# A decoder step on one Trainium2 core: the second norm's chain reordered, unread products in its wait, and the dt steps spaced out

## The chip, the core and the metric

The kernel runs as one program on one core of a Trainium2 chip. The core has five engines with instruction queues of their own: TensorE (PE; its weight loads are shown as PEld), VectorE (DVE), ScalarE (ACT), GpSimd (POOL) and SyncE (SP, which here only starts transfers). They meet in on-chip memory (SBUF) and in eight accumulator banks (PSUM), and wait for one another by semaphores. The metric is the device time of one execution in microseconds. The kernel before took 1796.03 us, the median of 3 runs (1794.56 to 1798.4).

## What is computed

One step of a hybrid decoder layer for 256 prompt tokens and 64 sample tokens (8 sequences of 8), 320 columns in all, with model width 2048:

```python
h   = rms_norm(x, norm_mix_pre)
proj = h @ w_in                       # gate u, gate v, SSD z, SSD x/B/C, dt
mix = concat([gate(u, v), ssd(z, conv(xBC), dt)]) @ w_out
x   = x + rms_norm(mix, norm_mix_post)            # "second norm"
f   = conv_ffn(rms_norm(x, norm_ffn_pre))         # w_up, causal conv, gelu(g) * u, w_down
x   = x + rms_norm(f, norm_ffn_post)              # last norm
```

`rms_norm(x, w)` divides each token's row by the root of the mean of its squares (plus 1e-6) and scales by `w`. The SSD scan also returns its state for the prompt and for each sample sequence. All is in float32.

## The kernel before

Activations lie transposed, with 128 features on the partitions and the 320 tokens along the free axis, so the model width is sixteen blocks ("columns" k = 0 to 15 of `hT`, `acc`). Float32 precision is got from three products of a faster format: a weight slab `wraw` (128 x 1024) is loaded by SP, ScalarE casts it to its high part `whi` (L118), VectorE subtracts to get the low part `wlo` (L120), and `accumulate` (L127 to L131) issues whi x h_hi, whi x h_lo and wlo x h_hi, each 128 x 128 by 320 columns. Slabs, high and low parts have three buffers each; the next slab is loaded when both parts of an older one are made, and a part's buffer is free when PE has used it.

`project` (L153) multiplies `hT` by the columns of a weight matrix. Up to k = 12 it takes slabs of two k-blocks for four output blocks, and with `more` also slabs of four k-blocks for two more outputs (L191 to L193); so four k-blocks are 72 products. `chunk_out` (L205) multiplies one chunk of mixed features by `w_out` or `w_down` and adds the result to `acc` on VectorE (L217). `squares_of` (L284) squares each finished block and adds it to a running total; the last blocks go by VectorE, the very last stays by itself.

Around the second norm (L1013 to L1028) the order is written out by hand with `tc.issue_after`, which places an instruction behind another one in the order of its engine: behind the last product of the output projection come the two state products of `grown` (L834) with their additions (L836) and stores from POOL's queue (L841), the sums by token of the total and of the last square (`token_sums`, L263), the product of the prompt state (`final`, L938) with its addition (L940) and store (L941), the root and one Newton step (`rsqrt_by_root`, L249 to L255), and `spread` (L271), three transposes that bring the root back to the transposed layout.

`x1_ready` (L1037) is called by `project(ffn_w_up, ...)` one slab ahead. For each k it multiplies `acc` by the norm's weight and the spread root (L1042), adds the residual `xr` (L1043; on VectorE for k = 0 and 1, on POOL for the others), and splits the result into `h_hi` (ScalarE, L346) and `h_lo` (VectorE, L347). When `k % 4 == 3` it asks for the next block of the residual on SP. The third norm needs the squares of the new `acc` (L1051 to L1053), which VectorE adds up; their sums by token stand in PE's order behind the first product of `ps_one` (L1107 to L1115).

`steps` (L411) is a generator for the SSD's step sizes, ticked along with the projections: sums over the decay (`cs_ps` L473, `csT_ps` L488, `dec_ps` L501) follow the softplus of dt on VectorE (L449 to L465), with exponentials on ScalarE (L484, L510, L514). Between its yields, other work is put in.

A scheduler outside the kernel orders each engine's instructions by priority (`first()` and `high_priority` raise it) and by its own estimates, so a change at one place can reorder neighbours.

## Time and profile before

| | us |
|---|---|
| median of 3 runs | 1796.03 (1794.56 to 1798.4) |
| the profiled execution's own time | 1796.18 |
| its span, first to last instruction | 1794.3 |
| PE busy | 1774.6 |
| VectorE busy | 1185.2 |
| ScalarE busy | 797.8 |
| POOL busy | 293.2 |
| mean granted clock of TensorE | 0.996 |
| PE's longest waits: for the last norm's additions | 2.4 in 2 |
| for the second norm's first split | 2.1 in 1 |

In rows of a timeline the first number is the start from the beginning of the span, the second the length, then engine, line, operation, output and inputs with shapes; brackets hold the idle time ahead of it and what ended that. Neighbouring rows of one kind are merged (x2). In rows of windows the stretch is followed by its length, the busy time of the engines asked for with the number of instructions touching it, the granted clock of TensorE as a share of full, the share of time the transfer engines were busy, and GB/s. Products overlap on PE, so the spacing of their starts, and not their length, is what one costs.

### The profile page before, as it was taken

What the parts mean: (1) busy time and instruction counts of PE and PEld (TensorE: products, weight loads), DVE (VectorE), ACT (ScalarE), POOL (GpSimd) and SP (SyncE); (2) the same over time, 40 slices, a digit from 0 to 9 for tenths busy, and PEclk for the clock granted to TensorE, in tenths of its full rate; (3) what the DMA queues carried; (4) which work ended last, traced back from release to release, by engine and by line L of the source; (5) the groups of instructions that cost most, each with busy time, mean ns of one, the idle gap of its engine ahead of it and who ended that gap; (6) DMA issues with size and microseconds to landing.
All of it is one profiled execution on the core that took longest, in us unless ns stands there. A gap on an engine that the chain in (4) does not pass through costs nothing.

```text
span 1794.3 us, 31172 instructions
## 1 busy us (share of the span) xinstructions
PE 1774.6 (99%) x12200; PEld 1741.1 (97%) x12200; DVE 1185.2 (66%) x2048; ACT 797.8 (44%) x1107; POOL 293.2 (16%) x619
## 2 busy tenths in 40 slices
PE   9999999999999999999999999999999999999998
PEld 8999999999889898999999999999999999999997
DVE  5459664556987969677875474746566575656575
ACT  6444454334545446445555433343434343433335
POOL 3102200000431303104321010111101020101004
PEclk9999999999999999999999999999999999999999
DMA  8646544445665565554554545554554555454542
GB/s 279 193 142 192 161 145 153 154 153 180 198 196 187 166 222 163 172 170 145 167 156 154 151 147 155 154 151 148 155 153 146 152 155 152 149 150 154 153 150 101
DMA packets 222226, 292.56 MB, mean 163 GB/s; under 512 B 16672, under 2 KB 150656, under 8 KB 221888
## 3 DMA queue, kind: packets, MB, share of 16 engines
q1 hardware_dynamic: 209392, 268.12, 49.1%
q10 hardware_dynamic: 10304, 14.82, 2.3%
q0 software_dynamic: 2384, 7.64, 1.4%
q8 instruction: 96, 1.57, 0.4%
q14 instruction: 50, 0.41, 0.1%
HBM read 275.71 MB, written 14.82 MB: 162 GB/s over the span
## 4 chain that ended last, share of the span: by engine, by line
PE 91%; DVE 4%; DMA 3%; issue 1%; ACT 1%; POOL 0%; DVEq 0%; ACTq 0%; POOLq 0%
PE ps L129 20%; PE ps L131 19%; PE ps L130 19%; PE pd L129 9%; PE pd L131 9%; PE pd L130 9%; DMA wraw<-in_w_in 1%; DVE wlo L120 1%; DMA cs<-dacs_d 1%; PE y_ps L912 1%; PE yo_ps L817 0%; PE sg L670 0%; DVE cv L388 0%; PE up_ps L834 0%; DVE cs L897 0%
## 5 line engine op out<-in xcount | busy, mean ns | idle before, releaser
L120 DVE TENSOR_TENSOR wlo<-wraw,whi 128x1024 fp32r<-128x1024 f32 (+1 forms) x474 | 585.4, 1235 | 434.0 <-ACT whi L118 431.9
L118 ACT CAST whi<-wraw 128x1024 fp32r<-128x1024 f32 (+1 forms) x475 | 494.8, 1042 | 715.9 <-PE ps L130 431.5
L129 PE MATMUL ps<-h_hi,whi 128*128 128x320 f32 x2524 | 783.4, 311 | 4.8 <-ACT h_hi L346 2.1
L131 PE MATMUL ps<-h_hi,wlo 128*128 128x320 f32 x2524 | 781.3, 310 | 2.0 <-DVE wlo L120 1.9
L130 PE MATMUL ps<-h_lo,whi 128*128 128x320 f32 x2524 | 780.8, 309 | 0.0
L129 PEld LDWEIGHTS ps<-h_hi,whi 128*128 128x128 f32 x2524 | 475.1, 188 | 8.8 <-issue 2.9
L131 PEld LDWEIGHTS ps<-h_hi,wlo 128*128 128x128 f32 x2524 | 474.9, 188 | 3.8 <-DVE wlo L120 3.1
L130 PEld LDWEIGHTS ps<-h_lo,whi 128*128 128x128 f32 x2524 | 475.2, 188 | 0.7 <-DVE h_lo L546 0.2
L129 PE MATMUL pd<-fhi,whi 128*128 128x320 f32 x704 | 217.5, 309 | 0.0
L130 PE MATMUL pd<-flo,whi 128*128 128x320 f32 x704 | 217.5, 309 | 0.0
L131 PE MATMUL pd<-fhi,wlo 128*128 128x320 f32 x704 | 217.5, 309 | 0.0
L129 PE MATMUL pd<-ohi,whi 128*128 128x320 f32 x448 | 139.8, 312 | 0.0
L131 PE MATMUL pd<-ohi,wlo 128*128 128x320 f32 x448 | 138.8, 310 | 0.0
L130 PE MATMUL pd<-olo,whi 128*128 128x320 f32 x448 | 138.6, 309 | 0.0
L129 PEld LDWEIGHTS pd<-fhi,whi 128*128 128x128 f32 x704 | 132.4, 188 | 0.0
L130 PEld LDWEIGHTS pd<-flo,whi 128*128 128x128 f32 x704 | 132.4, 188 | 0.0
L131 PEld LDWEIGHTS pd<-fhi,wlo 128*128 128x128 f32 x704 | 132.4, 188 | 0.0
L1093 POOL COPY ptf<-pad 128x2 f32<-128x2 f32 x88 | 21.0, 239 | 622.3 <-DVE pad L1081 621.6
L217 DVE TENSOR_TENSOR acc_ffn<-acc_ffn,pd 128x320 f32<-128x320 f32 x160 | 77.5, 484 | 38.3 <-PE pd L131 36.9
L129 PEld LDWEIGHTS pd<-ohi,whi 128*128 128x128 f32 x448 | 84.1, 188 | 1.4 <-issue 0.6
L131 PEld LDWEIGHTS pd<-ohi,wlo 128*128 128x128 f32 x448 | 84.1, 188 | 0.5 <-issue 0.4
L130 PEld LDWEIGHTS pd<-olo,whi 128*128 128x128 f32 x448 | 84.1, 188 | 0.2
(301 smaller groups left out, 1590.3 us busy)
## 6 DMA issues: line engine op xcount, KB each, us to landing
wraw<-in_ffn_w_up SPq DMA_DIRECT2D x176, 512.0 KB, 3.7
wraw<-in_w_in SPq DMA_DIRECT2D x144, 512.0 KB, 3.7
wraw<-in_ffn_w_down SPq DMA_DIRECT2D x88, 512.0 KB, 3.5
wraw<-in_w_out SPq DMA_DIRECT2D x64, 512.0 KB, 3.5
st<-in_state_ssm SPq DMA_DIRECT2D x32, 256.0 KB, 4.1
out_ssm_state_sample<-st ACTq DMA_DIRECT2D x30, 256.0 KB, 3.5
cs<-dacs_d SPq DMA_DIRECT2D x16, 320.0 KB, 4.2
xr<-in_xT SPq DMA_DIRECT2D x4, 640.0 KB, 3.9
```

What stands on the lines that cost most here:

```text
L118: act.copy(hi[:, o], raw[:, o])
L120: dve.tensor_tensor(out=lo[:, :m], in0=raw[:, :m], in1=hi[:, :m].bitcast(F32), op=ALU.subtract)
L129: pe.matmul(ps, whi, xhi, start=first, stop=False)
L130: pe.matmul(ps, whi, xlo, start=False, stop=False)
L131: return pe.matmul(ps, wlo, xhi, start=False, stop=last).ins
L217: dve.tensor_tensor(out=acc[:, nb, :], in0=acc[:, nb, :], in1=ps[:, :NT], op=ALU.add)
L912: pe.matmul(ps[64 * i:64 * i + 64, cols], w(hl), x(hl, m, cpx), tile_position=(0, 64 * i), **flags)
L1093: pool.tensor_copy(ptf[:, k, :], pad[:, 256:258])
```

## The change

1. In `chunk_out`, where block 15 is added at the end of a norm's last chunk, the addition is made in two parts (tokens 0 to 127, 128 to 319), and `squares_of` squares the two parts one by one. It concerns the second and the last norm.
2. The two state products of the last SSD group and their additions are placed behind the second part. The addition of the prompt state and its store move from between root and residual to behind the low part of k = 2.
3. The parts of the slab that feeds outputs 4 and 5 of the up projection (cast and subtraction) are placed behind the root and behind the low part of k = 1.
4. One product of 128 x 128 by 512 columns, whose result nobody reads, is placed behind the prompt state's product, and seven more behind the spread.
5. k = 1 is multiplied only after k = 0's residual is added; all residual additions are on VectorE.
6. The first k-block of the up projection is taken by parts: four products with whi x h_hi, four with wlo x h_hi, then four with whi x h_lo.
7. `steps` yields five times, not two, ahead of the sums over the decay, and once more between them.

```diff
@@ slab
+            late = split_after[-1]
+            with tc.issue_after(late[0]) if late else nullcontext(), tc.issue_after(late[1]) if late else nullcontext():
+                hi = wp.tile([P, 1024], F32R, tag="whi", name="whi", bufs=3)
...
+                dve.tensor_tensor(out=lo[:, :m], in0=raw[:, :m], in1=hi[:, :m].bitcast(F32), op=ALU.subtract)
@@ project / part
-            by_part = range(nk if ready and k0 == 0 and nk == 1 else 0)
+            by_part = range(1 if ready and k0 == 0 and nk < 4 else 0)
             for k in by_part:
-                for i in range(3):
+                for i in (0, 1, 2) if nk == 1 else (0, 2, 1):
...
                     if more and k0 % 4 == 2:
+                        if k0 == 2:
+                            split_after.append((rooted[-1], low[1]))
                         with tc.issue_after(held[1]):
                             part(rows_of(w, k0 - 2, 4, more, 256), k0 - 2, 4, (4, 5))
+                        split_after.append(None)
@@ chunk_out
+    def parts_of(nb):
+        return (slice(0, P), slice(P, NT)) if nb == KD - 1 else (slice(0, NT),)
...
-                    dve.tensor_tensor(out=acc[:, nb, :], in0=acc[:, nb, :], in1=ps[:, :NT], op=ALU.add)
+                    for ts in parts_of(nb) if done else (slice(0, NT),):
+                        added_last[:] = [dve.tensor_tensor(out=acc[:, nb, ts], in0=acc[:, nb, ts], in1=ps[:, ts], op=ALU.add).ins]
@@ squares_of
-                act.activation((one or held)[-1], acc[:, nb, :], AF.Square)
+                for ts in parts_of(nb):
+                    act.activation((one or held)[-1][:, ts], acc[:, nb, ts], AF.Square)
@@ steps
-            yield
-            yield
+            for _ in range(5):
+                yield
...
                 act.activation(ed[s_at], p4[s_at, :, r], AF.Exp)
+            yield
@@ the second norm
+            def idle_products(ps, n):
+                for _ in range(n):
+                    ins = pe.matmul(ps, bsp[:, 0, :P], bsp[:, 0, :], start=True, stop=True).ins
+                return ins
...
-                with tc.issue_after(pd_last[-1]):
+                with tc.issue_after(pd_last[-1]), tc.issue_after(added_last[0]):
                     made = rest[0]()
...
                 behind = rsqrt_ins[-1]
-                with tc.issue_after(behind):
-                    next(rest[1])
+                idle = misc("idle")
+                with tc.issue_after(made):
+                    made = idle_products(idle, 1)
                 with tc.issue_after(made):
                     r2b = spread(r)
+                with tc.issue_after(spread_ins[-1]):
+                    idle_products(idle, 7)
@@ x1_ready
-                        dve.scalar_tensor_tensor(out=a, in0=a, scalar=col(prm_at["norm"][0] + kt), in1=r2b, op0=ALU.mult, op1=ALU.mult)
-                        added.append((dve if kt < 2 else pool).tensor_tensor(out=a, in0=a, in1=xr[q][:, k, :], op=ALU.add).ins)
-                        split(hT[0][:, kt, :], hT[1][:, kt, :], a, col(prm_at["norm"][1] + kt))
+                        with tc.issue_after(added[0]) if kt == 1 else nullcontext():
+                            dve.scalar_tensor_tensor(out=a, in0=a, scalar=col(prm_at["norm"][0] + kt), in1=r2b, op0=ALU.mult, op1=ALU.mult)
+                        added.append(dve.tensor_tensor(out=a, in0=a, in1=xr[q][:, k, :], op=ALU.add).ins)
+                        low.append(split(hT[0][:, kt, :], hT[1][:, kt, :], a, col(prm_at["norm"][1] + kt)))
...
             project(ffn_w_up, 0, None, late=up0, ready=x1_ready, after=behind, ahead=1, more=DFF, held=added)
+            with tc.issue_after(low[2]):
+                next(rest[1])
```

In the changed kernel's order of instructions PE has, behind the prompt state's product: one unread product, the three transposes, seven unread products, then the products of k = 0. POOL loses its 14 residual additions. ScalarE has the cast of the slab for outputs 4 and 5 behind the root instead of ahead of the last square, and two more table loads around the dt steps. SP has one more weight load ahead of the dt steps' stores, and two more ahead of the loads of the next convolution's rows. In front of the last squares of the third norm VectorE has three more weight subtractions than before.

More of the change, by code (lines that the diff above doesn't have):

```diff
@@ L106, in first @@
         return tc.high_priority(offset=200000)
-    slab_load = []
+    slab_load, split_after = [], [None]
     def slab(src, begins=False):
@@ L115, in slab @@
             slab_load.append(sp.dma_start(raw[:, :m].rearrange("p (a n) -> p a n", n=n), src).ins)
-            hi = wp.tile([P, 1024], F32R, tag="whi", name="whi", bufs=3)
-            for o in (slice(0, P), slice(P, m)) if begins else (slice(0, m),):
-                act.copy(hi[:, o], raw[:, o])
-            lo = wp.tile([P, 1024], F32R, tag="wlo", name="wlo", bufs=3)
-            dve.tensor_tensor(out=lo[:, :m], in0=raw[:, :m], in1=hi[:, :m].bitcast(F32), op=ALU.subtract)
+            late = split_after[-1]
+            with tc.issue_after(late[0]) if late else nullcontext(), tc.issue_after(late[1]) if late else nullcontext():
+                hi = wp.tile([P, 1024], F32R, tag="whi", name="whi", bufs=3)
+                for o in (slice(0, P), slice(P, m)) if begins else (slice(0, m),):
+                    act.copy(hi[:, o], raw[:, o])
+                lo = wp.tile([P, 1024], F32R, tag="wlo", name="wlo", bufs=3)
+                dve.tensor_tensor(out=lo[:, :m], in0=raw[:, :m], in1=hi[:, :m].bitcast(F32), op=ALU.subtract)
         def block(k, c):
@@ L202, in hybrid_step @@
     acc = None
-    pd_last = []
+    pd_last, added_last = [], []
+    def parts_of(nb):
+        return (slice(0, P), slice(P, NT)) if nb == KD - 1 else (slice(0, NT),)
     def chunk_out(w, ck, hi, lo, begins, done=None, rate=1):
@@ L239, in rsqrt_of @@
         return r
-    rsqrt_ins, sums_ins = [], []
+    rsqrt_ins, sums_ins, spread_ins, rooted, low = [], [], [], [], []
     def rsqrt_by_root(rest, ps, scale, rows=P):
@@ L250, in rsqrt_by_root @@
         dve.scalar_tensor_tensor(out=v, in0=ps, scalar=scale, in1=v, op0=ALU.mult, op1=ALU.add)
-        act.activation(s, v, AF.Sqrt)
+        rooted.append(act.activation(s, v, AF.Sqrt).ins)
         dve.reciprocal(r, s)
@@ L270, in spread @@
         for c, o in ((2, NT - P), (0, 0), (1, P)):
-            pe.transpose(ps[:, o:o + P], r[:, c:c + 1].to_broadcast([P, P]), ident)
+            spread_ins.append(pe.transpose(ps[:, o:o + P], r[:, c:c + 1].to_broadcast([P, P]), ident).ins)
         if out is not None:
@@ L343, in split @@
             act.copy(hi, x)
-            dve.tensor_tensor(out=lo, in0=x, in1=hi.bitcast(F32), op=ALU.subtract)
+            made = dve.tensor_tensor(out=lo, in0=x, in1=hi.bitcast(F32), op=ALU.subtract)
         else:
             act.activation(hi, x, AF.Copy, scale=scale)
-            dve.scalar_tensor_tensor(out=lo, in0=x, scalar=scale, in1=hi.bitcast(F32), op0=ALU.mult, op1=ALU.subtract)
+            made = dve.scalar_tensor_tensor(out=lo, in0=x, scalar=scale, in1=hi.bitcast(F32), op0=ALU.mult, op1=ALU.subtract)
+        return made.ins
     def out_parts(pool_, name):
```

## The prediction

> **What bounds the kernel now.** I read the page first, then the list of who waited for whom, then the granted clock by stretches, and last the timeline around the stretch where TensorE stands still.
>
> ```profile
> PE 1774.6 (99%) x12200; PEld 1741.1 (97%) x12200; DVE 1185.2 (66%) x2048; ACT 797.8 (44%) x1107; POOL 293.2 (16%) x619
> ```
> ```profile
> PE ps L129 <- ACT h_hi L346: 2.1, 1, 2.1
> ```
>
> TensorE is busy through 99% of the span, so only three things can shorten the kernel: fewer products, fewer stops of PE, or a faster clock in between. One stop of 2.1 us stands out: the first products of the up projection wait for the first split of the second norm's output. What it costs is more than 2.1 us, as the windows show (columns: PE, PEld, DVE, ACT, POOL busy, then the granted clock):
>
> ```profile
> 838.99:842.40 3.41, 2.20 (x11) 1.13 (x11) 2.56 (x10) 0.20 (x1) 1.58 (x3) 1.00 0.49 183
> 842.40:845.81 3.41, 2.21 (x8) 2.21 (x9) 3.41 (x8) 2.50 (x6) 1.11 (x1) 0.50 0.20 77
> 845.81:849.23 3.42, 3.42 (x15) 3.42 (x14) 2.98 (x6) 2.18 (x6) 3.02 (x3) 0.50 0.33 72
> 849.23:852.64 3.41, 3.41 (x25) 3.41 (x24) 3.41 (x6) 1.61 (x3) 1.17 (x2) 1.00 0.67 238
> ```
>
> The clock falls to 0.50 at 842.40 and comes back at 849.23, two stretches of 3.41 us later. The products of the second stretch fill it completely, but at half clock. Their spacing is seen here, the first pair ahead of the norm, the second behind it:
>
> ```profile
> 837.04 0.31 PE L130 MATMUL pd<-h_lo,whi 128*128 128x320 f32 x1
> ...
> 837.18 0.31 PE L131 MATMUL pd<-h_hi,wlo 128*128 128x320 f32 x1
> ```
> ```profile
> 845.64 0.47 PE L131 MATMUL ps<-h_hi,wlo 128*128 128x320 f32 x1
> 845.90 0.47 PE L129 MATMUL ps<-h_hi,whi 128*128 128x320 f32 x1
> ```
>
> One product per 0.147 us (0.14 to 0.15 in the rows) against one per 0.267 us. By the Trainium skill ("TensorE: Matmul & The Clock Gate", "Why this matters for your kernels") only PE gaps above some 3 us drop the clock. The trace disagrees: the gap was 2.09 us and the fall came 0.9 us into it; by the page's rule only the gap would be there to win and the sum would end near 1795.2; the rows leave that no chance.
>
> **The chain of the norm, step by step.** First VectorE and ScalarE by themselves, then PE:
>
> ```profile
> 837.53 0.49 DVE L217 TENSOR_TENSOR acc_mix<-acc_mix,pd 128x320 f32<-128x320 f32 x1
> 837.93 1.28 DVE L836 TENSOR_TENSOR st<-st,up_ps 128x512 f32<-128x512 f32 x2
> 839.13 0.15 DVE L249 TENSOR_SCALAR rs_v<-tsum 128x3 f32<-128x3 f32 x1
> 839.72 0.16 DVE L250 SCALAR_TENSOR_TENSOR rs_v<-tsum,rs_v 128x3 f32<-128x3 f32 x1 [0.44 <-PE tsum L263]
> ...
> 840.83 0.68 DVE L940 TENSOR_TENSOR s<-s,fin_ps 128x512 f32<-128x512 f32 x1
> 841.55 1.01 DVE L1042 SCALAR_TENSOR_TENSOR acc_mix<-acc_mix,prm,spread 128x320 f32<-128x320 f32 x2
> 842.47 0.89 DVE L1043 TENSOR_TENSOR acc_mix<-acc_mix,xr 128x320 f32<-128x320 f32 x2
> ```
> ```profile
> 837.38 1.05 ACT L118 CAST whi<-wraw 128x1024 fp32r<-128x1024 f32 x1 [0.33 <-PE pd L130]
> 838.34 0.46 ACT L300 ACTIVATE sq<-acc_mix 128x320 f32<-128x320 f32 x1
> 839.91 0.20 ACT L251 ACTIVATE rs_s<-rs_v 128x3 f32<-128x3 f32 x1 [1.11 <-DVE rs_v L250]
> 842.99 1.01 ACT L346 ACTIVATE h_hi<-acc_mix,prm 128x320 fp32r<-128x320 f32 x2 [2.87 <-DVE acc_mix L1043]
> ```
> ```profile
> 837.33 0.62 PE L834 MATMUL up_ps<-xsp,bm 128*128 128x512 f32 x2
> ...
> 839.54 1.10 PE L938 MATMUL fin_ps<-xde,btok 128*128 128x512 f32 x2
> ...
> 840.97 0.54 PE L271 MATMUL spread<-ident,rs_r 128*128 128x128 f32 x3 [0.32 <-DVE rs_r L255]
> ...
> 843.61 0.63 PE L129 MATMUL ps<-h_hi,whi 128*128 128x320 f32 x1 [2.09 <-ACT h_hi L346]
> ```
>
> *Last block in parts, cast behind the root.* The addition of block 15 becomes 128 and 192 columns, and so does its square. An operation on 3 columns takes 0.16, so of the 0.49 some 0.15 is fixed; the parts take about 0.29 and 0.35, and with the overlap of 0.09 seen between 837.53 and 837.93 the second ends at 838.08 instead of 838.02. The cast of 1.05 no longer stands ahead of the square. Its last part then ends near 838.45, not 838.80, and the sums by token are there 0.35 earlier. But the two state additions (1.28) remain on VectorE ahead of the root's input; shifted by 0.06 they end at 839.27, the first small operation follows, the second at about 839.40 instead of 839.72. Gain **0.32**; bounds 0 (the second instruction costs more) and 0.35. The cast now waits for the root and ends by 840.8; behind it on ScalarE stands the first split, due at 842.3.
>
> *First product in the wait.* fin_ps moves up with the sums and is issued through by about 840.3; one 512-column product behind it ends by 840.6, and the spread is due at 840.65. Cost 0; if fin_ps is not earlier, 0.3.
>
> *Prompt state addition moved away.* Its 0.68 ends at 841.51, just when the spread (840.97 + 0.54) ends too, so moving it alone gives nothing; left there, it would have eaten the 0.32. On POOL's queue its store now waits some 30 us longer; behind it stand only the memsets and copies for the next convolution's pads, needed after the third norm. Cost 0.
>
> *Column 1 behind column 0's addition.* Before, two multiplications precede the first addition, which starts 0.92 behind the first of them (841.55, 842.47). Now it follows one, of 0.55 (half of 1.01 and the overlap), and a hand-over of 0.04 (839.72 + 0.16 to 839.91): **0.33** gained. The split, then PE, follow at the old distances (0.52, 0.62): PE begins real products at 842.96, not 843.61, which is 0.65 in all.
>
> *Seven unread products.* They start when the spread has been issued, about 841.1. By columns one takes 512/320 of 0.147, that is 0.235; seven take 1.64 and end at 842.75, inside the wait. Half of the pair's 0.62 is the upper bound: 2.17, ending at 843.27, 0.3 late. I take the lower, since 0.62 contains the end of the last one once.
>
> **The clock.** With them the stretch up to 842.40 holds fin_ps, the spread and six of the eight wide products. I take it that the clock stays at 1.00. Before, 23 products stand in the two slow windows, some counted twice; about 21 are issued by 849.23. Now (849.23 - 842.96)/0.147 gives 43. The lead of 22 products is 3.2 us: **0.65** from the chain and **2.55** from the clock. Whether the fall is avoided hangs on what counts as activity; a stretch with less busy time kept its clock:
>
> ```profile
> 159.73:163.15 3.42, 2.13 (x15) 1.00 0.50 150
> ```
>
> Those were wide products, while the 2.20 at 838.99 were largely sums of one column, and transposes. The Trainium skill (same page, "Part 4: PE-mode transpose") says that transposes don't count as activity, and (Part 1) that the stretches run free of the kernel. By that a run whose stretch ends near 841.3 would still fall; it is the first rival below.
>
> **What is late next: VectorE.** The sixteen residual additions are all on VectorE now (two were). Rows of the stretch 842 to 872, and of one operation alone:
>
> ```profile
> L347 DVE SCALAR_TENSOR_TENSOR h_lo<-acc_mix,prm,h_hi 128x320 fp32r<-128x320 f32 x16 | 11.8, 761 | 1.0 <-ACT h_hi L346 1.0
> L120 DVE TENSOR_TENSOR wlo<-wraw,whi 128x1024 fp32r<-128x1024 f32 x6 | 9.9, 1652 | 0.4 <-ACT whi L118 0.4
> L1042 DVE SCALAR_TENSOR_TENSOR acc_mix<-acc_mix,prm,spread 128x320 f32<-128x320 f32 x16 | 8.0, 540 | 0.0
> ```
> ```profile
> 849.93 1.00 DVE L347 SCALAR_TENSOR_TENSOR h_lo<-acc_mix,prm,h_hi 128x320 fp32r<-128x320 f32 x2
> 850.86 0.99 DVE L1042 SCALAR_TENSOR_TENSOR acc_mix<-acc_mix,prm,spread 128x320 f32<-128x320 f32 x2
> ```
> ```profile
> 872.70 1.21 DVE L120 TENSOR_TENSOR wlo<-wraw,whi 128x1024 fp32r<-128x1024 f32 x1
> ```
> ```profile
> L1043 POOL TENSOR_TENSOR acc_mix<-acc_mix,xr x14: 864/1109/1857, 843.9 to 868.2; 128x320 f32<-128x320 f32 x14
> ```
>
> Added: 14 x 0.45 = 6.2 us. Removed: the stretching beside POOL's additions, 16 x (0.76 - 0.50) + 6 x (1.65 - 1.21) = 6.8. So VectorE's load stays as it is, and each column also loses POOL's 1.1 us on the way to its split. Per four columns VectorE needs 4 x (0.50 + 0.45 + 0.50) + 3 x 1.21 = 9.4 us; PE consumes 72 products in 10.6. It keeps up, but PE comes 3.2 us earlier, and the margin is thin once: PE reaches columns 4 and 5 at 842.96 + 72 x 0.147 = 853.5, and VectorE, beginning at 841.23, has by then 8 multiplications, 8 additions, 6 low parts and 2 weights to do, 13.0 us with full durations, 854.2; rows that overlap by 0.08 each take off 1.9. A second thin place is the third norm's sum:
>
> ```profile
> 881.61 1.68 DVE L282 TENSOR_TENSOR sq<-sq,sq 128x320 f32<-128x320 f32 x3
> ```
> ```profile
> 888.74 0.72 PE L263 MATMUL tsum<-ones,sq 128*128 128x1 f32 x6
> ```
>
> 5.4 us of slack before. Now PE is there at 842.96 + 289 x 0.147 = 885.4, three more weight splits (3.6) stand ahead of the last squares, so these end at about 885 to 887. I charge **0.2** for both places; bounds 0 and 1.6.
>
> **The dt steps.**
>
> ```profile
> 239.48 0.33 DVE L465 SCALAR_TENSOR_TENSOR sp_e<-dt,a_bc 128x160 f32<-128x160 f32 x1
> ...
> 239.86 0.41 PE L473 MATMUL cs_ps<-sp_e,upper 128*128 128x32 f32 x2 [0.40 <-DVE sp_e L465]
> ```
> ```profile
> 245.62 1.05 ACT L118 CAST whi<-wraw 128x1024 fp32r<-128x1024 f32 x1 [1.88 <-PE ps L130]
> 246.69 1.28 ACT L338 ACT_TABLE_LOAD   x1
> ```
>
> Three ticks more between the decay and its sums remove the **0.40**. The products are the same. The exponentials now stand between the gate's activations: two more table loads of 1.28 on ScalarE, which waits 1.88 for PE here; covered. The last two sums wait for POOL's mask, whose buffer frees behind an activation, several us ahead of PE. If that cover fails: up to 1.3 lost. On SP the decay's stores now follow one more weight load each, and the loads of the next convolution's rows two; those rows are needed only after the third norm.
>
> **The last norm** takes the parts too; its sums waited 0.36 on the square:
>
> ```profile
> 1778.11 0.52 PEld L263 LDWEIGHTS tsum<-ones,sq 128*128 128x128 f32 x4 [0.36 <-ACT sq L300]
> ```
>
> There x1p's product already fills PE until shortly before, so I take **0.1**; bounds 0 and 0.36.
>
> **Sum.** The profiled run took 1796.18 (span 1794.3 and 1.9 around it), 0.15 above the median 1796.03. 1796.18 - 0.65 - 2.55 - 0.40 - 0.10 + 0.2 = **1792.7**. With one term at its bound it is 1792.4 to 1794.4 (dt steps +1.7), with all good ones 1792.2, all bad ones 1796.8.
>
> **Rivals.**
> 1. *The clock falls all the same.* For: 2.20 busy us didn't hold it. Against: eight wide products add 1.9 us of dense work. Fallen at 841.3 to 842, the unread products stretch by 0.267/0.147 and end 1.1 late, and the real ones run at half clock for about another 1.1 us, losing 0.6: 1.7 given back, **1794.4**. This is also the case that the change doesn't do what it says.
> 2. *VectorE becomes the bound; slower than before.* If low parts and weights keep the means of the group rows (0.76, 1.65) without POOL beside them, four columns need 4 x (0.54 + 0.49 + 0.76) + 3 x 1.65 = 12.1 us against PE's 10.6, and PE waits 4 x 1.5 = 6.0: **1798.7**. It decides from 11.5 us per four columns on (4 x 0.9 equals the 3.5 gained). For: windows with VectorE busy 3.41 of 3.41. Against: the single rows of 0.50 and 1.21 where POOL rests.
> 3. *The squares or the dt steps are late*: both covers fail, 1.4 and 0.4 + 0.4 lost, **1794.9**.
>
> **Chances.** Forecast 0.62 (own range 1791.3 to 1794.2); rival 1 0.17; rival 2 0.09; rival 3 0.12. A measurement of this kernel can tell about 0.2%, 3.6 us, from no change: faster is below 1792.4, slower above 1799.6. The forecast lies just on the near side of that bound: 0.36 of its 0.62 below it, and 0.02 of the others, so faster 0.38; slower 0.04, from the far part of rival 2; same 0.58. The range runs from 1790.8 (no stall, a gain at the tail in full, the three runs of before spread by 3.8) to 1796.2 (both smaller rivals and most of the bad bounds together).
>
> **What would show it.** Right: clock 1.00 from 838 to 890, first real product near 842.96, PE waits for wlo and for the sum of sq3 under 0.3, wlo near 1.2 and low parts near 0.5 throughout, cs_ps without a wait. Wrong: a window at 0.50 behind 841; unread products at 0.43 apiece; PE waiting for wlo at columns 4 to 7; VectorE rows still stretched with POOL idle; tsum waiting for sq3 above 1 us.

## The result and the profile after

The changed kernel takes **1791.59 us** (median of 22 runs, 1787.43 to 1794.75), the kernel before 1794.52 on the same occasion (median of 22, 1790.32 to 1798.85). The ratio is **0.9985**, 95% interval 0.9978 to 0.9992: a gain of 0.15%, about 2.7 us, where 3.5 had been forecast and 1792.7 given. A second set of the changed kernel gave 1792.56 and a ratio of 0.9988 (0.9979 to 0.9997). So the time came out close to the number, though the kernel before came out 1.5 lower here than the 1796.03 on which the number was built. The way to it did not, and that is what the rest is about. The profiled execution of the changed kernel took 1794.75 us, the longest of its 22, with a span of 1792.8.

PE's line of the page, and its longest waits, which answer to those of before:

```profile
PE 1774.8 (99%) x12208; PEld 1740.8 (97%) x12208; DVE 1184.6 (66%) x2064; ACT 800.4 (45%) x1111; POOL 278.0 (16%) x605
```
```profile
PE tsum L273 <- DVE sq L292: 2.0, 1, 2.0
...
PE ps L168 <- ACT whi L120: 0.3, 1, 0.3
```

The wait of 2.1 for the first split is gone; so is the 0.4 for `cs_ps`. A new one of 2.0 stands at the top: the third norm's sums over tokens wait for their squares. What each did to the clock is seen in windows (columns as before), cut at the edges at which the clock changed in this execution:

```profile
833.37:836.78 3.41, 3.41 (x27) 3.31 (x25) 3.30 (x8) 1.01 (x3) 0.00 (x0) 1.00 0.48 139
836.78:840.19 3.41, 2.99 (x15) 1.97 (x15) 2.19 (x9) 1.14 (x2) 1.12 (x2) 1.00 0.55 207
840.19:843.60 3.41, 3.27 (x21) 2.79 (x20) 3.41 (x9) 1.89 (x5) 0.00 (x0) 1.00 0.00 0
884.57:887.98 3.41, 2.12 (x16) 2.12 (x17) 2.28 (x8) 0.12 (x1) 0.00 (x0) 1.00 0.59 166
887.98:891.39 3.41, 3.41 (x15) 3.37 (x15) 1.69 (x8) 0.00 (x0) 0.00 (x0) 0.50 0.44 128
```

The second norm keeps full clock, as forecast. Then, 45 us later, PE stands still in the window from 884.57 and the clock falls in the next one. The half clock has moved from the second norm to the third.

To see what that was worth, the span is cut at four products that both kernels have, the first dt product, the last product of the gate, the spread of the last gated norm, and the first product of the last norm:

```profile
187.21 0.31 PE L426 MATMUL ps_dt<-h_hi,whi_dt 128*64 128x320 f32 x1
...
432.05 0.33 PE L671 MATMUL sg<-wS,vt 128*128 128x64 f32 x2
...
791.24 0.49 PE L271 MATMUL spread<-ident,rs_r 128*128 128x128 f32 x3
...
1777.48 0.78 PE L1164 MATMUL x1p<-acc_mix,ident 128*128 128x320 f32 x2
```

and in the changed kernel:

```profile
186.57 0.31 PE L439 MATMUL ps_dt<-h_hi,whi_dt 128*64 128x320 f32 x1
...
431.32 0.33 PE L685 MATMUL sg<-wS,vt 128*128 128x64 f32 x2
...
789.24 0.49 PE L281 MATMUL spread<-ident,rs_r 128*128 128x128 f32 x3
...
1776.07 0.79 PE L1190 MATMUL x1p<-acc_mix,ident 128*128 128x320 f32 x2
```

The differences of these starts, for every profile that was taken, are in the table. *Start* is up to the first dt product and holds nothing of the change; *dt* is from there to the gate's last product; *middle* up to the spread, again without the change; *norms* from the spread to the last norm and holds all the rest but the last norm itself. *Wait* is PE's wait for the third norm's squares (where it says none, the weight loads of these sums may still have waited a little: 0.33 in "no unread products", 0.21 in "chain as before"); *half clock* names the places at 0.50 ahead of the tail.

| kernel | start | dt | middle | norms | wait | half clock |
|---|---|---|---|---|---|---|
| before | 187.21 | 244.84 | 359.19 | 986.24 | none | second norm, 6.8 us |
| before, again | 187.70 | 246.33 | 359.17 | 986.29 | none | dt, 3.4; second norm, 6.8 |
| changed | 186.57 | 244.75 | 357.92 | 986.83 | 2.0 | third norm, 3.4 |
| changed, again | 187.32 | 244.76 | 357.84 | 986.99 | 2.2 | third norm, 3.4 |
| no unread products | 185.80 | 244.75 | 357.99 | 984.87 | none | second norm, 3.4 |
| squares ahead | 186.95 | 244.75 | 358.52 | 983.08 | none | none |
| squares ahead, no products | 184.78 | 244.78 | 357.57 | 985.40 | none | second norm, 6.8 |
| dt as before | 187.33 | 246.42 | 357.15 | 983.64 | 0.3 | dt, 3.4 |
| state behind squares | 186.25 | 244.74 | 356.92 | 983.71 | 0.3 | none |
| chain as before | 186.97 | 244.76 | 356.95 | 984.72 | none | second norm, 3.4 |
| additions on POOL | 185.45 | 244.77 | 359.16 | 985.79 | none | none |
| dt sums together | 184.79 | 244.58 | 357.08 | 984.58 | 1.2 | none |
| both mends | 184.54 | 244.75 | 357.01 | 984.17 | 0.6 | none |
| best | 186.23 | 244.56 | 357.63 | 983.11 | none | none |

Read the first and the third line: of the 1.54 us between their last products, 0.64 come from the start and 1.27 from the middle, which the change doesn't touch; dt gives 0.09, the last norm 0.13, and the stretch with nearly all of the change is **0.59 longer**. In the second pair it is 0.70 longer, and dt gives 1.57. The start varies by 3.2 us over the fourteen profiles and the middle by 2.3, with the same order of instructions in them; this is the noise in which a median of 12 runs of this kernel stands, and why the stretches, and not the medians, decide below.

### The profile page after: what moved, and what is told of

Same layout as the page of the kernel before. It is cut to its first block, busy times and chain, and to the rows that moved or that the text cites. A ratio compares the mean times of both kernels' runs of the same rounds, so it can differ in the third digit from the quotient of the medians.

```text
span 1792.8 us, 31196 instructions
## 1 busy us (share of the span) xinstructions
PE 1774.8 (99%) x12208; PEld 1740.8 (97%) x12208; DVE 1184.6 (66%) x2064; ACT 800.4 (45%) x1111; POOL 278.0 (16%) x605
## 3 DMA queue, kind: packets, MB, share of 16 engines
q8 instruction: 96, 1.57, 0.4%
## 4 chain that ended last, share of the span: by engine, by line
PE 91%; DVE 4%; DMA 3%; issue 1%; ACT 0%; POOL 0%; DVEq 0%; SPq 0%; ACTq 0%; POOLq 0%
PE ps L131 19%; PE ps L133 19%; PE ps L132 19%; PE pd L131 10%; PE pd L133 10%; PE pd L132 10%; DVE wlo L122 1%; DMA wraw<-in_w_in 1%; PE y_ps L931 1%; DMA wraw<-in_ffn_w_up 1%; DMA cs<-dacs_d 1%; PE yo_ps L836 1%; PE up_ps L853 0%; PE sg L684 0%; DVE acc_mix L1066 0%
## 5 line engine op out<-in xcount | busy, mean ns | idle before, releaser
L227 DVE TENSOR_TENSOR acc_ffn<-acc_ffn,pd 128x320 f32<-128x320 f32 (+1 forms) x161 | 77.4, 481 | 38.0 <-PE pd L133 36.7
```

The costliest lines, as they stand in the source:

```text
L227: added_last[:] = [dve.tensor_tensor(out=acc[:, nb, ts], in0=acc[:, nb, ts], in1=ps[:, ts], op=ALU.add).ins]
```

## The experiments

The question was where the expected 3 us of the second norm went. *Theory A*: the clock is kept and the chain is shorter, as forecast; but PE then reaches the third norm's sums before its squares are there, waits, and the clock falls at that wait. *Rivals*: the products do nothing; or what was won is simply in the total and the third norm's wait costs nothing.

**No unread products.** The lines with `idle_products` are left out; the order is otherwise the same on every engine.

```diff
-                idle = misc("idle")
-                with tc.issue_after(made):
-                    made = idle_products(idle, 1)
...
-                with tc.issue_after(spread_ins[-1]):
-                    idle_products(idle, 7)
```

> The changed kernel without its eight unread products; the order on every engine is otherwise the same. Theory A (the clock is kept by the products, but what they win is given back at the third norm, where the sum waits 2.0 us for late squares and the clock then falls): two stretches of 3.41 us at 0.50 come back behind the second norm, PE reaches the third norm's sum some 2.5 us later, the wait for its squares goes from 2.0 to under 0.5 and the clock stays at 1.00 there; time within 1.5 us of the changed kernel's 1791.6. Rival B (the prediction's sum, in which the clock is worth 2.55 to the end): 1794.1. Rival C (the products do nothing for the clock): no stretch at 0.50 behind the second norm, same time.

Measured: 1790.78 us (12 runs), ratio 0.9987 (0.9979 to 0.9995). The windows of the norm:

```profile
837.89:841.30 3.41, 1.53 (x10) 1.29 (x11) 2.74 (x7) 1.40 (x4) 0.00 (x0) 1.00 0.27 99
841.30:844.71 3.41, 3.41 (x15) 3.41 (x14) 3.41 (x9) 2.02 (x5) 0.00 (x0) 0.50 0.22 27
```

The clock falls again, for one window where theory A had two, so rival C is out; PE's wait for the squares is gone and the norms take 1.96 us *less* than in the changed kernel, so rival B is out too. Theory A holds in kind: 1.4 us lost at the second norm, not 2.5 (first real product to the block of one column 43.88 us instead of 42.51), buy back 3.2 at the third (from that block's first product to its spread 4.54 instead of 7.78). Not all of this is PE's later arrival: the squares themselves end 0.5 earlier behind the first real product (44.2 instead of 44.7).

**Squares ahead.** The first weight split behind the up projection is placed behind the third norm's squares (`squared` collects the squares and additions).

```diff
+            squared = []
             with tc.issue_after(added[15]):
                 for kt in range(KD):
-                    add_square(sq3, acc[:, kt, :], kt < 1, dve, ("pv", 4))
+                    squared += add_square(sq3, acc[:, kt, :], kt < 1, dve, ("pv", 4))
...
                 for i in range(2):
+                    split_after.append((squared[-2], squared[-1]) if i == 0 else None)
                     wb = slab(rows_of(ffn_w_up, 8 * i, 8, DFF + 256, P))
```

> The changed kernel with the first weight split behind the up projection held back until the third norm's squares and their additions are issued. Theory A: the sum over tokens waits under 0.3 us instead of 2.0, the clock stays at 1.00 from 880 to 895, and the time is 3 to 3.6 us below the changed kernel: about 1788.3. Rival B: PE comes earlier to the evacuation, whose reciprocal root starts little earlier, and the wait for pad grows from 1.2 to 3 or more: under 1.5 us gained, 1790.5. Rival C: the held split is late and PE waits 1 us or more for wlo: no gain.

Measured: 1791.22 us (12 runs), ratio 0.9984 (0.9974 to 0.9993). On VectorE and PE:

```profile
876.41 6.44 DVE L292 TENSOR_TENSOR sq<-sq,sq 128x320 f32<-128x320 f32 x11
882.77 2.35 DVE L122 TENSOR_TENSOR wlo<-wraw,whi 128x1024 fp32r<-128x1024 f32 x2
```
```profile
884.55 0.72 PE L273 MATMUL tsum<-ones,sq 128*128 128x1 f32 x6
```

Eleven additions in one row end at 882.85, the sums follow without a wait, and the splits behind them are still in time. The norms take 983.08, 3.75 less than in the profile of the changed kernel and 3.16 less than before: this is the gain that had been forecast for them. The wait for `pad` stays at 1.2 (rival B is out). The median misses theory A's 1788.3: it is only 0.4 below the changed kernel's first set and 1.3 below its second, inside the noise.

**Squares ahead, no products.** Both edits.

> Both edits: squares ahead of the split, and no unread products. Theory A: the price of the second norm's clock by itself, with nothing late behind it to hide it: 2.5 us above the run with the squares ahead alone, about 1790.8. Rival: if the later wait for pad decides, under 1 us above it.

Measured: 1791.43 us (12 runs), ratio 0.9988 (0.9978 to 0.9998). With nothing late behind it the fall of the clock costs the norms 985.40 - 983.08 = **2.3 us** (two windows), so theory A's 2.5 is borne out by the stretches. The medians differ by only 0.2, as the rival had it, but that is less than they can tell (this profile alone reached the dt products 2.2 earlier than the other, ahead of every edit).

**dt as before.** Two ticks instead of five, none behind the exponentials.

```diff
-            for _ in range(5):
-                yield
+            yield
+            yield
...
-            yield
```

> The changed kernel with the dt steps spaced as in the kernel before (two ticks, none behind the exponentials). Theory A: the wait of 0.4 us for the sums of the decay comes back and nothing else, 0.4 us above the changed kernel, 1792.0. Rival B: the wait of 0.9 us for a mixer addition, which the kernel before has near 508 us and the changed one has not, comes back with it: 1.3 above, 1792.9. Rival C: nothing is lost, the wait is covered elsewhere.

Measured: 1792.06 us (12 runs), ratio 0.9996 (0.9986 to 1.0006). The wait of 0.4 came back, but the stretch grew by 1.67, more than any theory had: the clock fell. The second profile of the kernel before shows the same (PE's rows, then windows):

```profile
240.34 0.63 PE L473 MATMUL cs_ps<-sp_e,upper 128*128 128x32 f32 x4 [0.41 <-DVE sp_e L465]
...
242.70 0.63 PE L508 MATMUL dec_ps<-sp_e,later_s 64*128 64x32 f32 x4
```
```profile
240.12:243.53 3.41, 3.19 (x26) 2.74 (x27) 2.38 (x7) 1.34 (x2) 0.00 (x0) 0.99 0.47 148
243.53:246.94 3.41, 3.41 (x14) 3.41 (x14) 0.30 (x2) 0.38 (x3) 0.00 (x0) 0.50 0.31 114
```

The first window is 3.19 us busy and the clock falls all the same: 24 of its 26 products are sums over the decay with 32 to 128 columns. Of the three profiles with these steps two fell, of the eleven with five ticks none. The table excludes rival B: the middle took 357.15 here.

**The changed kernel again**, without an edit.

> The changed kernel once more, for a second profile. The stretch from the last gated norm's spread (near 791 us) to the first product of the last norm took 986.24 in the kernel before and 986.83 in the changed one, but 983.64 in the run with the dt steps as before, which is the same kernel in that stretch; its weights landed sooner there. Theory A (the third norm's squares are late by as much as the weight loads beside the prompt state's store are slow): between 983.6 and 986.9, with a wait for the squares between 0.2 and 2.0 us, and the median within 1 us of 1791.6. Rival: 986.8 each time, with a wait of 2.0, so that the difference lies in the dt steps.

Measured: 1792.56 us (12 runs), ratio 0.9988 (0.9979 to 0.9997); norms 986.99, wait 2.2, both a little above theory A's range and as the rival had them. But "dt sums together" below, with the same order there, had a wait of 1.2. In these four profiles, what goes with the wait is the length of one weight load. In the chain that ended last in the changed kernel, between 866 and 891 us (start, length, what):

```profile
871.01 7.49 DMA wraw<-in_ffn_w_up
878.57 1.06 ACT whi L120
879.66 1.23 DVE wlo L122
...
885.86 0.83 PE tsum L273 x6
```

The same row of the chain in the second profile, in "dt sums together" and in "dt as before":

```profile
871.57 7.77 DMA wraw<-in_ffn_w_up
```
```profile
867.70 7.11 DMA wraw<-in_ffn_w_up
```
```profile
872.22 6.12 DMA wraw<-in_ffn_w_up
```

Loads of 7.77, 7.49, 7.11 and 6.12 us go with waits of 2.2, 2.0, 1.2 and 0.3. The rival is not borne out: with the dt steps as changed the same load took 6.2 in "no unread products" and 6.3 in "squares ahead". Why it varies stays open. ScalarE stands at the cast of that slab with five squares of the norm queued behind it. Usually such a load takes 3.7 us (the median of the page). What lies beside it is in POOL's rows:

```profile
871.87 0.54 POOL L960 DMA_DIRECT2D out_ssm_state_prompt<-s  x1 [33.76 <-DVE s L959]
```

the prompt state's store of 256 KB, which the change moved here. The transfers started between 866 and 878 us, with their number, size and median time to landing, in the changed kernel:

```profile
wraw<-in_ffn_w_up SPq DMA_DIRECT2D x4, 512.0 KB, 5.4
out_ssm_state_prompt<-s POOLq DMA_DIRECT2D x1, 256.0 KB, 5.6
```

**State behind squares.** Addition and store of the prompt state go behind the last square instead of behind the low part of k = 2 (`squared` is collected as above); PE's order stays.

```diff
-            with tc.issue_after(low[2]):
-                next(rest[1])
...
+            with tc.issue_after(squared[-1]):
+                next(rest[1])
```

> The changed kernel with the prompt state's last addition and its store, which it moved from the second norm's chain to the time of the last weight splits, moved on behind the third norm's squares; PE's order is the same. Theory A (the moved addition of 0.68 us and the store of 256 KB beside three weight loads make the squares late): wait for the squares under 0.3 us, stretch from 791 us to the last norm near 983.2, time 0.5 to 3 us below the changed kernel. Rival (PE being 3 us earlier is enough to make them late): the wait stays at 1 us or more, 984.5 to 986.8.

Measured: 1790.62 us (11 runs), ratio 0.9983 (0.9974 to 0.9993). The load in the chain, the load that stands in the place of the 7.49 (the third of four), POOL's store, and PE:

```profile
865.30 3.56 DMA wraw<-in_ffn_w_up
```
```profile
wraw<-in_ffn_w_up SPq DMA_DIRECT2D x1, 512.0 KB, 5.8
```
```profile
883.01 0.54 POOL L960 DMA_DIRECT2D out_ssm_state_prompt<-s  x1 [46.22 <-DVE s L959]
```
```profile
882.77 0.83 PE L273 MATMUL tsum<-ones,sq 128*128 128x1 f32 x6 [0.35 <-DVE s L959]
```

The wait is 0.35, a little over theory A's bound, and is put down to the state's addition itself, the last on VectorE; the norms take 983.71 where 983.2 was expected. PE's lead is as it was, 42.4 us from the first real product to the block of one column, and the squares end 42.4 us behind that product, just in time. So in this profile the rival is out: the lead alone doesn't make them late.

How much the moved addition and store do is not settled by it. In the four profiles whose loads are listed above, with both in place, the squares end 42.9 us behind the first real product where the load took 6.12, 43.8 where it took 7.11, and 44.7 and 44.9 where it took 7.49 and 7.77. Against the first of these the edit wins 0.5, about the 0.68 of the addition. The rest goes with the length of the load, and that the store sets it is not shown. In the changed kernel the slow load is the third of four started 3.0, 1.1 and 2.0 us apart; the first of them took 3.6 there too, and that first one is what the chain names here. The third took 5.8 here and 6.6 in "both mends", both times with the store far behind; with the store beside it, it took 6.0 to 7.8. So loads set this close together are slow without a store, and the two ranges overlap.

**Chain as before.** No parts, the cast not behind the root, column 1 not behind column 0's addition.

```diff
-        return (slice(0, P), slice(P, NT)) if nb == KD - 1 else (slice(0, NT),)
+        return (slice(0, NT),)
...
-                            split_after.append((rooted[-1], low[1]))
+                            split_after.append(None)
...
-                        with tc.issue_after(added[0]) if kt == 1 else nullcontext():
+                        with nullcontext():
```

> The changed kernel with the chain of the second norm as before: the last block not in parts, the cast not behind the root, column 1 not behind column 0's addition; unread products, additions and dt steps as changed. Theory A (the prediction's terms): from the first sum over tokens to the first real product 5.8 us instead of 5.29, with the clock still at 1.00 from the unread products; 0.5 above the changed kernel where the third norm's wait is the same, and that wait 0.5 shorter where it is not. Rival: the longer gap lets the clock fall in spite of the products; 2 us or more above.

Measured: 1791.16 us (11 runs), ratio 0.9984 (0.9975 to 0.9993). From the first sum to the first real product 6.77 us, not 5.8, and the rival's condition holds: the clock fell although the products are there.

```profile
835.26:838.67 3.41, 2.88 (x18) 1.96 (x17) 2.28 (x9) 1.19 (x3) 1.13 (x2) 1.00 0.67 247
838.67:842.08 3.41, 3.41 (x11) 2.73 (x10) 2.83 (x7) 1.39 (x4) 0.00 (x0) 0.50 0.10 38
```
```profile
838.86 3.33 PE L749 MATMUL idle<-bsp 128*128 128x512 f32 x7
```

The window up to 838.67 held state products, one-column sums and one unread product; the seven came behind its end, at half clock, and took 3.33 us instead of 1.86, so the real ones waited for them. The rest of the rival, 2 us or more above, did not come: the third norm's squares were in time, with PE later and the squares earlier (42.5 us behind the first real product instead of 44.7).

**Additions on POOL.** Fourteen of the residual additions back on GpSimd.

```diff
-                        added.append(dve.tensor_tensor(
+                        added.append((dve if kt < 2 else pool).tensor_tensor(
```

> The changed kernel with fourteen of the sixteen residual additions back on GpSimd. Theory A (the prediction's account: VectorE gains by their absence what it loses by stretched operations): low parts and weight splits between 842 and 868 us stretch again to 0.6 to 0.8 and 1.4 to 1.7 us, PE waits for none of it or under 1 us, and from the first real product to the single column block takes 42.4 to 43.4 us. Rival (the additions on VectorE are what makes the third norm's squares late): the wait for the squares falls from 2.0 to under 0.5 us. Rival B (PE, 3 us earlier, runs into GpSimd's additions): 2 us or more of waits for h_hi or wlo, clock falls.

Measured: 1791.73 us (11 runs), ratio 0.9996 (0.9987 to 1.0005). VectorE's groups from 842 to 868 us, here and, from 841 to 866, in the changed kernel:

```profile
L358 DVE SCALAR_TENSOR_TENSOR h_lo<-acc_mix,prm,h_hi 128x320 fp32r<-128x320 f32 x14 | 12.3, 897 | 0.3 <-ACT h_hi L357 0.3
L122 DVE TENSOR_TENSOR wlo<-wraw,whi 128x1024 fp32r<-128x1024 f32 x6 | 8.2, 1365 | 0.8 <-ACT whi L120 0.8
```
```profile
L122 DVE TENSOR_TENSOR wlo<-wraw,whi 128x1024 fp32r<-128x1024 f32 x6 | 7.3, 1215 | 0.4 <-ACT whi L120 0.4
...
L1067 DVE TENSOR_TENSOR acc_mix<-acc_mix,xr 128x320 f32<-128x320 f32 x15 | 6.6, 481 | 0.0
L358 DVE SCALAR_TENSOR_TENSOR h_lo<-acc_mix,prm,h_hi 128x320 fp32r<-128x320 f32 x12 | 6.1, 542 | 0.6 <-ACT h_hi L357 0.6
```

Low parts stretch from 0.54 to 0.90 and splits from 1.22 to 1.37. From the first real product to the block of one column PE needs 44.61 us instead of 42.51, the clock staying at 1.00: 2.1 us in stops of 0.1 to 0.3. That is more than theory A's 43.4 and what rival B named, but without one long wait and without a fall. The other rival is right as well: the wait for the squares is gone, and not only because PE comes 2.1 later. The last squares on VectorE, here and in the changed kernel:

```profile
878.45 2.87 DVE L292 TENSOR_TENSOR sq<-sq,sq 128x320 f32<-128x320 f32 x5
```
```profile
879.66 1.23 DVE L122 TENSOR_TENSOR wlo<-wraw,whi 128x1024 fp32r<-128x1024 f32 x1 [1.39 <-ACT whi L120]
...
884.73 1.08 DVE L292 TENSOR_TENSOR sq<-sq,sq 128x320 f32<-128x320 f32 x2
```

They end at 881.32 here and at 885.81 there, 40.1 and 44.7 us behind the first real product (39.7 in the kernel before), and would have been in time for a PE that came at 42.5. The prompt state's addition and store stand where the change put them. Nine weight splits are ahead of the last square, as in the kernel before, instead of twelve, and the three weight loads started between 866 and 878 us take 3.8 at the median with the store among them. By this run the additions on VectorE, with the order that comes with them, are the largest part of the squares' lateness: 4.6 us against this profile of the changed kernel, and 2.8 against "dt as before", whose load was the shortest.

With the norms at 985.79 the additions on VectorE are the better place by 2.7, once the squares are in time (983.08).

**dt sums together.** The sixth tick, behind the exponentials, is left out; the five stay.

> The changed kernel without the sixth tick, which parts the column sums from their transposed copies; the five ticks ahead stay. Theory A: the wait of 0.4 us went with the five ticks, but each further stop between weight products costs some 0.3 us of change-over, so the stretch from the dt products to the last gate product is 244.4 to 244.6 instead of 244.75, with the clock at 1.00. Rival: the exponentials come back into the way of the sums and PE waits again, 244.8 or more, or 246.3 where the clock falls at it as in the second profile of the kernel before.

Measured: 1790.52 us (11 runs), ratio 0.9987 (0.9978 to 0.9996); dt 244.58 instead of 244.75, inside theory A's range, at full clock.

**Both mends.** Squares ahead of the split and the state behind the squares.

> The changed kernel with both mends of the third norm: the squares ahead of the next weight split, and the prompt state's addition and store behind the squares. Theory A: no wait for the squares, clock 1.00 there, stretch from 791 us to the last norm 983.0 to 983.3, as with the squares ahead alone (983.08), since nothing of the wait is left to win; median 1790 to 1791 and about 0.2% below the kernel before. Rival: with store and loads apart, PE also stops waiting for pad: 982.5 or less.

Measured: 1791.60 us (11 runs), ratio 0.9991 (0.9982 to 1.0000). A miss: norms 984.17, with a wait of 0.6 which is again put down to the state's addition, as it ends up behind two splits. In these profiles one mend is better than two. The load in the place of the 7.49 took 6.6 with the store started 14 us later:

```profile
wraw<-in_ffn_w_up SPq DMA_DIRECT2D x1, 512.0 KB, 6.6
```

**The kernel before again**, without an edit.

> The kernel before once more, for a second profile. Theory A: behind 841 us the clock falls again, for one or two stretches of 3.41 us as their phase has it, and the stretch from 791 us to the last norm is 985 to 986.5. What it had between 431 and 791 us, 1.3 us more than the changed kernel, is not of the change and may be gone. Rival: the 1.3 us come back, and are then the change's doing (the dt steps move the stores on the load queue).

Measured: 1798.20 us in its one execution. The clock fell at the second norm again, for two windows, and the norms took 986.29 as in the first profile; it also fell at the dt steps, as shown above. The middle took 359.17, so the rival's 1.3 us came back. But "additions on POOL" has 359.16 with the changed kernel's order in it, and "dt as before" 357.15 with the order of before; so it is not the change's doing as far as these fourteen profiles tell, and why both profiles of before have it stays open.

**Best.** Squares ahead, and the dt sums together.

> The changed kernel with the squares ahead of the next weight split, and without the sixth tick of the dt steps. Theory A (the stretches add up): from the dt products to the last gate product 244.6 us, from 791 us to the last norm 983.1, no wait for squares, clock 1.00 up to the tail; by stretches 3.4 us below the kernel before where its clock held at the dt steps and 4.9 where it fell, median 1789.5 to 1790.5. Rival: the two edits move weight loads against each other and one of the two stretches is 0.5 us or more longer than in the run that had its edit alone.

Measured: **1789.97 us** (12 runs), ratio **0.9981** (0.9970 to 0.9991), against 1792.12 for the kernel before on the same chip; dt 244.56, norms 983.11, no fall ahead of the tail. The stretches add up as theory A had it. That it is faster than the changed kernel is shown by the stretches only; the ratios' intervals overlap.

## Why the prediction held, and where it did not

The rows of the chain in the changed kernel, VectorE and then PE, for the first points:

```profile
835.53 0.55 DVE L227 TENSOR_TENSOR acc_mix<-acc_mix,pd 128x128 f32<-128x128 f32 x2
836.00 1.28 DVE L855 TENSOR_TENSOR st<-st,up_ps 128x512 f32<-128x512 f32 x2
837.19 0.15 DVE L259 TENSOR_SCALAR rs_v<-tsum 128x3 f32<-128x3 f32 x1
837.46 0.16 DVE L260 SCALAR_TENSOR_TENSOR rs_v<-tsum,rs_v 128x3 f32<-128x3 f32 x1
...
839.36 0.55 DVE L1066 SCALAR_TENSOR_TENSOR acc_mix<-acc_mix,prm,spread 128x320 f32<-128x320 f32 x1 [0.70 <-PE spread L281]
```
```profile
839.07 1.86 PE L749 MATMUL idle<-bsp 128*128 128x512 f32 x7
841.08 0.85 PE L168 MATMUL ps<-h_hi,whi 128*128 128x320 f32 x4
```

- *Last block in parts, cast behind the root, 0.32:* right. From the block's addition to the root's input 835.53 to 837.46, 1.93 us; before 837.53 to 839.72, 2.19. Gain 0.26.
- *Column 1 behind column 0's addition, 0.33:* right. From the first multiplication to the first real product 1.72 us (839.36 to 841.08) against 2.06: 0.34. Between the root's input and the first multiplication 0.07 was lost, so the chain as a whole gained 0.53 of the 0.65.
- *First and seven unread products, 0:* right. The seven end at 840.93, 0.15 ahead of the real ones. With the chain of before they did not even keep the clock; in all nine profiles with the chain and the products as changed it stayed at 1.00.
- *The clock, 2.55:* right in place and size. From the first real product to the block of one column 44.99 before, 42.51 now, 2.48; and by the two runs with the squares ahead 2.3 in the whole stretch.
- *VectorE's load stays as it is:* right as a sum, by the rows above and the page (1185.2 before, 1184.6 now); no wait for `wlo` at columns 4 and 5. The margin there was worked out from halves of merged rows, in which the overlap is already out, and then 1.9 was taken off for it once more; nothing came of it. The price of leaving the additions on POOL, 2.1 us once PE comes earlier, was not seen.
- *Third norm's sum and columns 4 and 5, 0.2, bounds 0 to 1.6:* **here the prediction failed.** The place was named, and PE's arrival was right: it had been worked out as 885.4 - 842.96 = 42.4 us behind the first real product, and it came 42.5 behind it. The squares were later than the bound: they end at 885.81, which is 44.73 us from the first real product where the prediction had 42.0 to 44.0. Against the kernel before they end 5.0 us later behind that product. Three more splits are 3.6, which the prediction had; it did not have the moved addition (0.68) and the wait of 1.39 for a slab that took 7.49; together 5.7, a little more than was lost. With the additions back on POOL nearly all of this goes, with the state moved on a part. PE waited 2.0 and 2.2 us in the two profiles, where the prediction had named a wait above 1 us as a sign of being wrong, and behind the wait the clock fell for one window: 7.78 us from the block's first product to the spread instead of 4.20, **3.6 us** for 0.2. The prediction itself had priced a stop of 2.09 us at twice its length, by the fall of the clock; that price was used for the gain and not for the loss. The third rival had the mechanism and gave it 1.4.
- *Prompt state addition moved away, 0:* too low. It was priced by what stands behind its store on POOL's queue, and not by the squares behind it on VectorE, which it puts off by its 0.68. The store was waited for, too: SP's queue held the next convolution's rows back 4.0 us for it, which is not on the chain shown.

```profile
SPq L1093 <- DMA out_ssm_state_prompt<-s: 4.0, 1, 4.0
```
- *dt steps, 0.40:* too low where it counts and too high where it was measured. The wait went, but two stops instead of one cost change-overs, so at full clock only 0.09 was left (0.26 with the sums together). The worth of the ticks is the fall of the clock that they prevent, 1.5 to 1.6 us (246.33 and 246.42 against 244.84) in two of three profiles. The first profile of the kernel before, on which the sum was made, was the one without the fall.
- *Last norm, 0.10:* right, 10.05 to 9.92 from its first product on.

So the total was met with the third norm's loss put 3.4 too low and, in executions where the clock had fallen at the dt steps, their gain put 1.2 too low. That it came so near the forecast is luck as far as this goes, since the two errors have opposite signs. The rest can only be argued: both profiled executions of the changed kernel lie near the upper end of their sets, and with a load of 6 us in place of 7.5 the norms would take some 3 us less (983.64 in "dt as before"). How often the load takes 7 us was not measured, so the exact make-up of the 2.7 us stays open. Shown is that in both profiles of the change the norms were longer than before, and that they were 2.5 to 3.2 us shorter than before with the addition and store or the squares moved.

On the clock, the Trainium skill ("TensorE: Matmul & The Clock Gate", Part 1) has the window run free of the kernel and speaks of how busy PE is. The traces agree on the first (with the same dt steps and the same stop of 0.4 us the clock fell in two executions and held in a third), and on the second only if busy is not read off the profile: after 3.19 us of 3.41 in narrow products it fell, after 2.13 in wide ones at 159.73 it did not.

## What to carry to other kernels

Here a stop of TensorE of some 2 us cost about twice its length, because the clock fell behind it. So a change that brings an engine forward has to be followed to the next place where its inputs have little slack, and a wait there is to be priced with the fall of the clock. Work that is moved off the critical chain or to another engine lands in front of something else; look for what stands in order behind it, and for loads that are then started close together. When a kernel's executions spread by more than the effect, cut the span at products that both versions have and compare the stretches.

## What was not expected of the hardware

- Narrow products did not hold the clock in two of three profiles: a window of 3.41 us that was busy for 3.19 by the profile, with 24 of 26 products of 32 to 128 columns, was followed by one at 0.50.
- Of four 512 KB loads started 3.0, 1.1 and 2.0 us apart the first took 3.6 us; the third took 5.8 and 6.6 without a store beside it and 6.0 to 7.8 with one of 256 KB.
- Seven unread products of 512 columns took 1.86 us at full and 3.33 at half clock: there the filler came behind the end of a thin window and added to the loss.
- VectorE's low parts on 320 columns went from 0.54 to 0.90 us with additions on GpSimd beside them, weight splits from 1.22 to 1.37; its multiplications of the same width stayed at 0.54.
